# Output stores moved and spaced, attention masks put after the exponential on another engine, and filter taps cast once: one change to an eight-core decoder step

## The chip, the cores and the metric

The kernel runs as one program on all 8 cores of one Trainium2 chip; each core does its own eighth of the tokens. The time is the device time of the slowest core, in microseconds (us). Cores 0 to 3 are one die and cores 4 to 7 the other.

Most executions of one kernel agree within 0.3%. Some fall in a second, slower state, in which the cores of one die (sometimes of both) show a lower granted TensorE clock. Only fast runs are compared here. Where a profile fell in the slow state, the text says which die was undisturbed and uses that one alone.

Engine names in the profile: PE is TensorE, PEld its weight loads, DVE is VectorE, ACT is ScalarE, POOL is GpSimd, SP is SyncE; a q after an engine means its sequencer.

## The reference, cut to what matters

One layer of a hybrid decoder: sliding-window attention with sinks and a gated depthwise convolution run in parallel on the same normed input, are merged by gates, and an MLP follows.

```python
n = rmsnorm(h, norm1_g)
q, k, v, u, g = project(n, w_in)            # u: gated (GLU), 1024 channels
ya = sink_attention(q, k, v)                # blocks of 128 queries see own + previous block
yc = swish(layernorm(depthwise_conv31(u))) @ w_conv_o
h  = h + (g0 * (ya @ w_attn_o) + g1 * yc) @ w_out
h  = h + relu(rmsnorm(h, norm2_g) @ w_up)**2 @ w_down
y  = rmsnorm(h, norm_f_g)
# two request groups: 2 x 8192 prompt tokens, and 128 x 4 sample tokens with KV and conv caches
```

## The kernel before

Each core handles 2048 prompt tokens and 64 sample tokens in three groups (groups 0, 1 and 2 below; 5, 6 and 5 blocks of 128 tokens, the last with the sample tokens). The stages of a group are: k/v/q projections; a loop over 8 channel tiles with the gated projection (`glu`) of tile m and the convolution of tile m-1; gates and branches; output projection; MLP. Work of other kinds is put between the matmuls as side tasks, one for each call of `step()`: the attention units in the conv loop, the next group's first norm in the MLP, and the final norm and the y stores of a group in the k/v/q stage of the next.

A helper records every operation with what it reads and writes, and derives the waits. It tracks SBUF in pieces of 128 bytes, but a DRAM tensor as one whole. So two stores into one output tensor are ordered: the second waits for the landing of the first, on the engine that issues it.

```python
def keys(self, ap):
    name = ap.tensor.name
    if name not in self.base:
        return [name]                  # a DRAM tensor: one key
    ...                                # SBUF: one key for each 128 bytes

# y stores of the group before, one side task each, between the k/v/q matmuls
def out(k):
    if k < 16:
        stt(H[:, k, 0:M], H[:, k, 0:M], v1(V_GF + k), LR[:, 0:M], ALU.mult, ALU.mult)
    if k > 0:
        P.dma("act", yo[g][:, k - 1, :], H[:, k - 1, 0:M], f"d_y{k - 1}")

# scores of an attention unit: the mask is added in PSUM by a product with the identity
for blk in range(2):
    ...
    for hh in range(2):
        b = bank()
        P.op("pe", "matmul", inc=False, out=b[:, :], lhsT=idb[:, :], rhs=msk[...], start=True, stop=False)
        bb.append(b)
    for hh in range(2):
        P.op("pe", "matmul", out=bb[hh][:, :], lhsT=kT[...], rhs=qo[...], start=False, stop=True)
    for hh in range(2):
        act(p[:, :], bb[hh][:, :], AF.Exp, scale=SCALE)

def unit(i, a):                        # scores of this unit, values of the one before
    r = scores(i, a)
    if prev[0]:
        values(*prev[0])
    prev[0] = (i, a, r)

# ... cut ...
def glu(m):
    u = um[m % 3]
    wl = slab()                        # next 1 MB of weights, loaded on GpSimd's queue
    for ci, (c0, n) in enumerate(UC):  # two chunks of columns
        bB = fm(wl, 0, nT, us + c0, n) # 16 matmuls
        step(ci == 0)                  # a unit here in chunk 0
        bA = fm(wl, 1, nT, us + c0, n)
        ...                            # tanh on ACT, product on DVE, into u
        step(ci == 1)                  # and a unit here in chunk 1
    z = ush[m % 2]
    for i in range(4):
        for q in range(4):             # 16 shifted copies, each with its own semaphore
            P.dma("sp", z[32 * i:32 * i + 32, q, 0:L - 3], u[32 * q:32 * q + 32, i:i + L - 3],
                  f"d_ul{m % 2}{i}{q}", merge=(i + q > 0))

def conv(m):                           # 64 small matmuls (96 in the last group)
    z = ush[m % 2]
    P.dma("pool", c_w[:, :, :, :], cwd[m]..., "d_cw")   # taps, cast while loaded
    ...
for m in range(8):
    glu(m)
    if m >= 1:
        conv(m - 1)
```

The taps, the conv temporaries and, in the last group, the sample caches (`KcT`, `vcb`) and the conv state (`stb`) lie in SBUF over the rows of `H` that the y stores still read, so they can be loaded only when those rows have been stored. The caches' loads stand ahead of the last conv loop.

The softmax here doesn't subtract the row's maximum and nothing guards it: scores larger than these inputs give would overflow.

## Time and profile before

| | us |
|---|---|
| median of 4 runs (two of them slow) | 3645.57 (3559.49 to 3942.81) |
| most of its fast runs, over all the rounds below | 3558 to 3592 |
| profiled execution, slowest core | 3556.6 |
| mean span of the 8 cores in it | 3548.2 |

The page of the kernel before begins with busy time by engine; of the 40 slices of the span I show PE's busy tenths and the granted clock.

```profile
span 3556.6 us, 61094 instructions; the slowest of 8 cores (3539.9 to 3556.6 us)
...
PE 3376.2 (95%) x23732; PEld 2172.0 (61%) x23732; DVE 1162.6 (33%) x1846; ACT 705.5 (20%) x1381; POOL 202.3 (6%) x371
...
PE   2999999999999999999999999987999999999994
...
PEclk9999999999999999999999999998999999999997
```

TensorE is the limit. It is idle for 180 us, at the start, in the tail, and in the k/v/q stage of the last group (the 8 and the 7). The list of PE's waits says on whom; its columns are total us, number of times, and the longest.

```profile
PE ps L154 <- DVE R_58 L154: 63.2, 2, 32.8
PE ps L154 <- ACT qo L154: 31.3, 6, 9.1
PE ps L154 <- DMA ush_83<-um_93: 11.1, 3, 5.9
PE ps L154 <- ACT vtok L154: 8.0, 2, 7.0
PE ps L154 <- ACT vst L154: 6.3, 1, 6.3
...
PE ps L154 <- DMA ush_82<-um_93: 2.9, 2, 2.2
```

`R_58` is the first norm. `qo` and `vtok` are the copies of q and v out of PSUM on ACT. What held ACT is in the list of all waits, and its timeline in group 1 shows the pattern (start, us, instruction, and in brackets the idle time before it and who ended it):

```profile
ACT qo L154 <- DMA y<-H: 68.8, 14, 12.8
...
ACT vtok L154 <- DMA y<-H: 45.0, 7, 10.6
```

```profile
1120.92 0.38 ACT L154 ACTIVATE vtok<-ps 128x256 bf16<-128x256 f32 x1 [1.36 <-PE ps L154]
1128.82 0.34 ACTq L154 DMA_DIRECT2D y<-H  x1
1129.26 0.38 ACT L154 ACTIVATE vtok<-ps 128x256 bf16<-128x256 f32 x1 [7.96 <-DMA y<-H]
1139.83 0.34 ACTq L154 DMA_DIRECT2D y<-H  x1
1140.27 0.38 ACT L154 ACTIVATE vtok<-ps 128x256 bf16<-128x256 f32 x1 [10.63 <-DMA y<-H]
```

Each y store sits on ACT until the store before has landed, and the copy behind it waits along. TensorE runs out of PSUM banks and idles, and the granted clock in these stretches is lower, as a table by stretch of these two k/v/q stages shows (the column after POOL is the granted clock):

```profile
1110.00:1190.00 80.00, 65.15 (x399) 40.12 (x397) 16.61 (x18) 10.54 (x25) 2.64 (x5) 0.89 0.63 143
2335.00:2440.00 105.00, 74.19 (x457) 47.20 (x456) 22.17 (x23) 14.95 (x37) 6.76 (x11) 0.84 0.73 157
```

Last, PE's timeline of one attention unit and the convolution after it, in group 0 (core 4).

```profile
189.07 0.59 PE L154 MATMUL ps<-msk,idb 128*128 128x512 bf16 x2
189.59 0.39 PE L154 MATMUL ps<-qo,kT 64*128 64x512 bf16 x2
189.92 0.60 PE L154 MATMUL ps<-msk,idb 128*128 128x512 bf16 x2
190.46 0.39 PE L154 MATMUL ps<-qo,kT 64*128 64x512 bf16 x2
...
191.76 2.38 PE L154 MATMUL ps<-ush_82,cw 128*32 128x320 bf16 x64
```

### The profile page before, as it was taken

The numbers are of one execution on the slowest core, as the hardware profiler recorded it, in microseconds if no ns is written. First come the engines' busy times: TensorE is split into PE (matmuls) and PEld (weight loads), VectorE is DVE, ScalarE is ACT, GpSimd is POOL, SyncE is SP. The second block draws the span as 40 slices with busy tenths as digits, with TensorE's granted clock in tenths as the row PEclk, the third lists the DMA queues.
The fourth block names the chain that finished last, engine by engine and source line by source line (L and its number), as shares of the span: only waits on it lengthen the run. The fifth ranks groups of instructions, "written<-read, shape, count | busy, mean of one in ns | idle before, by whom it ended". The sixth has DMA issues, their size and how long they took to land.

```text
span 3556.6 us, 61094 instructions; the slowest of 8 cores (3539.9 to 3556.6 us)
## 1 busy us (share of the span) xinstructions
PE 3376.2 (95%) x23732; PEld 2172.0 (61%) x23732; DVE 1162.6 (33%) x1846; ACT 705.5 (20%) x1381; POOL 202.3 (6%) x371
## 2 busy tenths in 40 slices
PE   2999999999999999999999999987999999999994
PEld 1656777777776455666666666654566666666663
DVE  4244133332223354224233222333542242222224
ACT  2322133111021333113211011112231131101021
POOL 0000000000000000000000000001100000000000
PEclk9999999999999999999999999998999999999997
DMA  6779877887666666556666655567776666566661
GB/s 135 118 133 174 161 149 152 161 167 136 119 122 134 125 130 143 106 115 118 137 131 132 122 99 104 101 138 156 142 153 114 126 110 113 107 112 114 108 114 71
DMA packets 98474, 453.52 MB, mean 128 GB/s; under 512 B 14960, under 2 KB 27696, under 8 KB 55472
## 3 DMA queue, kind: packets, MB, share of 16 engines
q0 software_dynamic: 51696, 355.75, 56.5%
q1 hardware_dynamic: 39584, 76.56, 8.0%
q10 hardware_dynamic: 6912, 17.30, 1.3%
q8 instruction: 195, 3.19, 0.4%
q14 instruction: 87, 0.71, 0.1%
HBM read 765.00 MB, written 23.85 MB: 222 GB/s over the span
## 4 chain that ended last, share of the span: by engine, by line
PE 89%; DMA 6%; SPq 2%; DVE 1%; issue 1%; ACT 0%; DVEq 0%; ACTq 0%
PE ps L154 89%; DMA y<-H 4%; SPq L154 2%; DMA H<-x 1%; DMA ush_83<-um_93 0%; DVE H L154 0%; DVE rden_67 L154 0%; DMA ush_82<-um_93 0%; DVE nT L154 0%; DVE LR L154 0%; DVE R_58 L154 0%; DMA ush_83<-um_94 0%; DVE um_93 L154 0%; DVE qo L154 0%; SPq L151 0%
## 5 line engine op out<-in xcount | busy, mean ns | idle before, releaser
L154 DVE TENSOR_TENSOR H<-ps,H 128x320 f32<-128x320 f32 (+2 forms) x384 | 201.5, 525 | 566.4 <-PE ps L154 566.2
L154 PE MATMUL ps<-nT,wsl_49 128*128 128x384 bf16 (+2 forms) x1344 | 217.9, 322 | 19.4 <-ACT qo L154 16.9
L154 PE MATMUL ps<-a2T,wsl_50 128*128 128x320 bf16 (+2 forms) x1344 | 203.9, 313 | 0.0
L154 PE MATMUL ps<-hb,wsl_53 128*128 128x320 bf16 (+2 forms) x1344 | 203.9, 313 | 0.0
L154 PE MATMUL ps<-a2T,wsl_51 128*128 128x320 bf16 (+2 forms) x1344 | 203.9, 313 | 0.0
L154 PE MATMUL ps<-hb,wsl_52 128*128 128x320 bf16 (+2 forms) x1344 | 203.9, 313 | 0.0
L154 PEld LDWEIGHTS ps<-nT,wsl_49 128*128 128x128 bf16 x1344 | 133.3, 100 | 101.8 <-issue 33.9
L154 ACT ACTIVATE a2T<-rt_105 128x320 bf16<-128x320 f32 (+2 forms) x96 | 47.6, 496 | 736.1 <-DVE rt_105 L154 736.1
L154 PE MATMUL ps<-nT,wsl_50 128*128 128x352 bf16 (+2 forms) x1152 | 178.9, 316 | 8.6 <-ACT qo L154 8.6
L154 PE MATMUL ps<-nT,wsl_51 128*128 128x352 bf16 (+2 forms) x1152 | 178.2, 315 | 0.5 <-issue 0.5
L154 DVE SCALAR_TENSOR_TENSOR tA<-tA,ps 128x320 f32<-128x320 f32 (+2 forms) x96 | 50.0, 520 | 387.2 <-PE ps L154 386.7
L154 PE MATMUL ps<-hb,wsl_50 128*128 128x320 bf16 (+2 forms) x1152 | 175.3, 313 | 0.0
L154 PE MATMUL ps<-a2T,wsl_49 128*128 128x320 bf16 (+2 forms) x1152 | 174.8, 313 | 0.0
L154 PE MATMUL ps<-a2T,wsl_52 128*128 128x320 bf16 (+2 forms) x1152 | 174.8, 313 | 0.0
L154 PE MATMUL ps<-hb,wsl_51 128*128 128x320 bf16 (+2 forms) x1152 | 174.8, 313 | 0.0
L154 PE MATMUL ps<-a2T,wsl_53 128*128 128x320 bf16 (+2 forms) x1152 | 174.8, 313 | 0.0
L154 PE MATMUL ps<-hb,wsl_49 128*128 128x320 bf16 (+2 forms) x1152 | 174.8, 313 | 0.0
L154 PEld LDWEIGHTS ps<-hb,wsl_52 128*128 128x128 bf16 x1344 | 131.5, 98 | 69.4 <-issue 0.4
L154 PEld LDWEIGHTS ps<-a2T,wsl_50 128*128 128x128 bf16 x1344 | 131.5, 98 | 69.0
L154 PEld LDWEIGHTS ps<-hb,wsl_53 128*128 128x128 bf16 x1344 | 131.5, 98 | 69.0
L154 PEld LDWEIGHTS ps<-a2T,wsl_51 128*128 128x128 bf16 x1344 | 131.5, 98 | 69.0
L154 PE MATMUL ps<-nT,wsl_52 128*128 128x352 bf16 (+2 forms) x960 | 152.5, 320 | 14.3 <-ACT vtok L154 8.0
(222 smaller groups left out, 4284.0 us busy)
## 6 DMA issues: line engine op xcount, KB each, us to landing
wsl_49<-wst POOLq DMA_DIRECT2D x66, 1024.0 KB, 9.5
wsl_50<-wst POOLq DMA_DIRECT2D x66, 1024.0 KB, 9.5
wsl_51<-wst POOLq DMA_DIRECT2D x66, 1024.0 KB, 9.4
wsl_52<-wst POOLq DMA_DIRECT2D x66, 1024.0 KB, 9.8
wsl_53<-wst POOLq DMA_DIRECT2D x66, 1024.0 KB, 9.5
H<-x SPq DMA_DIRECT2D x8, 768.0 KB, 21.6
cw<-cwd POOLq DMA_DIRECT2D x24, 256.0 KB, 8.6
H<-x SPq DMA_DIRECT2D x16, 384.0 KB, 7.2
```

The costliest lines, as they stand in the source:

```text
L154: i = getattr(eng, ins[0])(**ins[1])
```

## The change

It has three parts. The y stores go from ACT to SyncE: eight at once in the side tasks, eight more one by one after each `glu`, in an order that frees the rows needed first; the sample caches are loaded only after tile 5 of the last loop. The 128 mask products on TensorE become 128 affine selects on GpSimd, which set masked exps to zero. The taps are cast to bf16 once, from DRAM to DRAM, and then loaded tile by tile by SyncE into two buffers. With this, the places of the attention units move: one at the end of each chunk, 32 matmuls apart, where they were 48 matmuls apart, then 16 and a convolution.

```diff
+Y_OUT = [0, 1, 2, 3, 4, 10, 11, 12, 5, 6, 7, 8, 9, 13, 14, 15]
@@ taps, behind the first five weight slabs on GpSimd's queue
+        cwb = nc.dram_tensor("cwb", [128, 8, 1024], BF16, kind="Internal").ap()
+        P.dma("pool", cwb[:, :, :], cwd[:, :].rearrange("p (m c) -> p m c", m=8), "d_cwb")
@@ y stores
-            def out(k):
-                if k < 16:
-                    stt(H[:, k, 0:M], H[:, k, 0:M], v1(V_GF + k), LR[:, 0:M], ALU.mult, ALU.mult)
-                if k > 0:
-                    P.dma("act", yo[g][:, k - 1, :], H[:, k - 1, 0:M], f"d_y{k - 1}")
+            def out(i, k):
+                stt(H[:, k, 0:M], H[:, k, 0:M], v1(V_GF + k), LR[:, 0:M], ALU.mult, ALU.mult)
+                stores.append(lambda: P.dma("sp", yo[g][:, k, :], H[:, k, 0:M], f"d_y{k}"))
+                if i < 8:
+                    store()
@@ masks
-                        P.op("pe", "matmul", inc=False, out=b[:, :], lhsT=idb[:, :],
-                             rhs=msk[...].unsqueeze(1).broadcast_to([128, 4, 128]), start=True, stop=False)
+                    bias = v1(V_HB) if first and i == 0 and blk == 0 else 0.0
...
-                        act(p[:, :], bb[hh][:, :], AF.Exp, scale=SCALE)
+                        act(p[:, :], bb[hh][:, :], AF.Exp, scale=SCALE, bias=bias)
+                        d = 1 if blk else -1
+                        v = p[:, :].rearrange("p (g q) -> p g q", g=4)
+                        P.op("pool", "affine_select", out=v, in_=v, pattern=[[0, 4], [d, 128]], base=blk - 1,
+                             channel_multiplier=-d, compare_op=ALU.is_ge, fill=0.0)
@@ conv loop
-                u = um[m % 3]
+                u = um[m % 2]
+                P.dma("sp", cw[m % 2][...], cwb[:, m, :]..., f"d_cw{m % 2}")
...
                     bB = fm(wl, 0, nT, us + c0, n)
-                    step(ci == 0)
                     bA = fm(wl, 1, nT, us + c0, n)
...
-                    step(ci == 1)
+                    step()
...
-                P.dma("pool", c_w[...], cwd[m]..., "d_cw")
...
             for m in range(8):
                 glu(m)
+                store()
+                if last and m == 5:
+                    sample_load()
```

More of the change, by code (lines that the diff above doesn't have):

```diff
@@ L26 @@
 NSLOT = 5
-V_G1, V_G2, V_GF, V_BG, V_CB, V_LG, V_LB, V_SK, V_N = 0, 16, 32, 48, 80, 88, 96, 104, 120
+V_G1, V_G2, V_GF, V_BG, V_CB, V_LG, V_LB, V_SK, V_HB, V_N = 0, 16, 32, 48, 80, 88, 96, 104, 120, 121
 G = 128
@@ L180, in build @@
         wst = din("wst", [110 * 128, 4096])
-        cwd = din("cwd", [8, 128, 1024])
+        cwd = din("cwd", [128, 8192])
         ck = din("ck", [16, 128, 256])
@@ L187, in build @@
         stT = din("stT", [128, 4096])
-        msd = din("msd", [128, 896])
+        msd = din("msd", [128, 512])
         ident = din("ident", [128, 128])
@@ L230, in build @@
         vec = sb("vec", [128, V_N], F32)
-        msk = sb("msk", [128, 896], BF16)
+        msk = sb("msk", [128, 512], BF16)
         idb = sb("idb", [128, 128], BF16)
@@ L249, in build @@
         gt = [over(H, i * 2048, f"gt{i}", [128, 512], F32) for i in range(2)]
-        cw = over(H, 4096, "cw", [128, 4, 8, 32], BF16)
-        um = [over(H, 6144 + i * 2560, f"um{i}", [128, ULEN], BF16) for i in range(3)]
+        cw = [over(H, 4096 + i * 2048, f"cw{i}", [128, 4, 8, 32], BF16) for i in range(2)]
+        um = [over(H, 8192 + i * 2560, f"um{i}", [128, ULEN], BF16) for i in range(2)]
         KcT = over(H, 5 * HB, "KcT", [128, 2, 16, 128], BF16)
@@ L372, in build, with store @@
                 stt(nT[:, k, c], H[:, k, c], v1(V_G1 + k), R1[:, c], ALU.mult, ALU.mult)
+        stores = []
+        def store():
+            if stores:
+                stores.pop(0)()
         def norm1_tasks(g):
@@ L397, in fin @@
                     rstd(LR, S2, c0, n)
-            def out(k):
-                if k < 16:
-                    stt(H[:, k, 0:M], H[:, k, 0:M], v1(V_GF + k), LR[:, 0:M], ALU.mult, ALU.mult)
-                if k > 0:
-                    P.dma("act", yo[g][:, k - 1, :], H[:, k - 1, 0:M], f"d_y{k - 1}")
-            return [fin] + [lambda k=k: out(k) for k in range(17)]
+            def out(i, k):
[3 more added lines that the diff above has]
+                    store()
+            return [fin] + [lambda i=i, k=k: out(i, k) for i, k in enumerate(Y_OUT)]
         for g, (b0, nb, halo, ns) in enumerate(GROUPS):
@@ L464, in scores @@
                 for blk in range(2):
-                    mi = 1 if blk else (0 if first and i == 0 else 2)
-                    bb = []
-                    for hh in range(2):
-                        b = bank()
-                        P.op("pe", "matmul", inc=False, out=b[:, :], lhsT=idb[:, :],
-                             rhs=msk[:, mi * 128:mi * 128 + 128].unsqueeze(1).broadcast_to([128, 4, 128]),
-                             start=True, stop=False)
-                        bb.append(b)
+                    bb = [bank(), bank()]
                     for hh in range(2):
@@ L475, in scores @@
                         P.op("pe", "matmul", out=bb[hh][:, :], lhsT=kT[hs, a, c0 + 128 * blk:c0 + 128 * blk + 128],
-                             rhs=qo[hs, a * 4:a * 4 + 4, c0:c0 + 128], start=False, stop=True)
+                             rhs=qo[hs, a * 4:a * 4 + 4, c0:c0 + 128], start=True, stop=True)
+                    bias = v1(V_HB) if first and i == 0 and blk == 0 else 0.0
                     for hh in range(2):
                         p = pt()
-                        act(p[:, :], bb[hh][:, :], AF.Exp, scale=SCALE)
+                        act(p[:, :], bb[hh][:, :], AF.Exp, scale=SCALE, bias=bias)
[3 more added lines that the diff above has]
+                             channel_multiplier=-d, compare_op=ALU.is_ge, fill=0.0)
                         res[hh, blk] = p
@@ L527, in sample_unit @@
                 pn, pc = pt(), pt()
-                P.op("pe", "matmul", inc=False, out=bn[0:64, 0:256], lhsT=idb[:, 0:64], rhs=msk[:, 640:896],
+                P.op("pe", "matmul", inc=False, out=bn[0:64, 0:256], lhsT=idb[:, 0:64], rhs=msk[:, 256:512],
                      start=True, stop=False)
@@ L532, in sample_unit @@
                 act(pn[0:64, 0:256], bn[0:64, 0:256], AF.Exp, scale=SCALE)
-                P.op("pe", "matmul", inc=False, out=bc[:, 0:256], lhsT=idb[:, :], rhs=msk[:, 384:640],
+                P.op("pe", "matmul", inc=False, out=bc[:, 0:256], lhsT=idb[:, :], rhs=msk[:, 0:256],
                      start=True, stop=False)
@@ L558, in build @@
             if last:
-                sample_load()
                 side += [sample_q] + [lambda a=a, hh=hh: sample_unit(a, hh) for a in range(2) for hh in range(2)]
@@ L573, in glu @@
             def glu(m):
-                u = um[m % 3]
+                u = um[m % 2]
                 wl = slab()
+                P.dma("sp", cw[m % 2][:, :, :, :], cwb[:, m, :].rearrange("p (b t c) -> p b t c", b=4, t=8), f"d_cw{m % 2}")
                 if not first:
@@ L612, in conv @@
                 z = ush[m % 2]
-                c_w = cw
+                c_w = cw[m % 2]
                 A = S1 if m == 0 else cf[m % 2]
-                P.dma("pool", c_w[:, :, :, :], cwd[m].rearrange("p (b t c) -> p b t c", b=4, t=8), "d_cw")
                 for c0, n in PC:
@@ L759, in build @@
         drain()
+        while stores:
+            store()
         P.emit()
@@ L826, in _prep_inputs @@
                 cwd[:, s, c32, :, t, c32] = cwt[j].reshape(8, 4, 32).transpose(2, 0, 1)
-    cwd = cwd.reshape(8, 128, 1024)
-    j = np.arange(128)[:, None]
-    i = np.arange(128)[None, :]
-    m_prev = np.where(j > i, 0.0, NEG).astype(np.float32)
-    m_own = np.where(j <= i, 0.0, NEG).astype(np.float32)
+    cwd = np.ascontiguousarray(cwd.reshape(8, 128, 1024).transpose(1, 0, 2).reshape(128, 8192))
     col = np.arange(256)[None, :]
@@ L836, in _prep_inputs @@
     m_cache = np.where(np.arange(128)[:, None] >= (col % 4) + 1, 0.0, NEG).astype(np.float32)
-    common = dict(ident=np.eye(128, dtype=np.float32), vecs=vecs, cwd=cwd,
+    common = dict(msd=np.concatenate([m_cache, m_new], 1), ident=np.eye(128, dtype=np.float32), cwd=cwd,
                   wst=_slabs(f(w_in)[0], f(w_attn_o)[0], f(w_conv_o)[0], f(w_out)[0], f(w_up)[0], f(w_down)[0]))
@@ L855, in _prep_inputs @@
         d.update(
-            msd=np.concatenate([m_prev if qd > 0 else np.full((128, 128), NEG, np.float32), m_own, m_prev,
-                                m_cache, m_new], 1),
+            vecs=np.where((np.arange(V_N) == V_HB)[None, :] & (qd == 0), np.float32(NEG), vecs),
             ck=np.ascontiguousarray(cK.reshape(16, 128, 256)), cv=np.ascontiguousarray(cV.reshape(16, 128, 256)),
```

## The prediction

> All times are for the fast state (profiled execution of before: 3556.6 us).
>
> **What bounds it now.** TensorE: the page gives PE 95% busy, the chain of waits is 89% PE. Of 180 us of PE idle, 63 us is the first norm and x load, about 45 us the tail. The rest, from the list of PE's waits: 31.3 us on ACT's qo copies, 14.3 on its v copies (vtok 8.0, vst 6.3), about 17 on the shifted conv copies (ush).
>
> **Y stores.** In the timelines of the k/v/q stage of groups 1 and 2, ACT sits between evictions behind its y stores, 2.2 to 13 us apart. Each waits for the landing of the one before: the program tracks a DRAM output as one whole. ACT cannot evict, the PSUM banks fill, PE stops, and the granted clock falls (0.89 and 0.84 in these windows). From the first k matmul to the first mask product: 86.8 us in group 1, 101.8 in group 2; the same matmuls at the undisturbed rate (163, 149, 109 ns for 384, 352, 256 columns) make 66.3 and 62.1. So 60 us is lost. SyncE keeps the chain of landings, but nobody waits for it there. I expect nearly all 60 us back. The final tail (16 stores, 2.3 us each) stays.
>
> **Masks.** In PE's timeline a unit's scores take 1.71 us, 1.07 of it mask products: 32 units, 34 us off a busy PE.
>
> **Added: 128 affine selects on GpSimd** between exp and values. A GpSimd tensor_scalar of 128x512 takes 1.49 us here; the Trainium skill, "GPSIMD Engine Reference", section 3.1, gives 0.77 us for a tight 512-element loop. I estimate 1.2 us. From a unit's scores to its values PE has about 6 us in group 0, 7 in group 1; four selects plus the first exp need about 6. Up to 1.4 us each it hides; at 2 us it would cost some 40 us. Expected loss: 6 us.
>
> **Conv taps.** The loads leave the GpSimd queue, where they waited 89 us for PE, but slab loads never held PE: no gain. The one cast stands behind the first five slabs and ends before the next is needed: 0 us. On SyncE, taps and y stores share the queue with ush copies, whose 16 issues take 10.6 to 12.7 us per channel tile, nearly a loop without attention units. I expect ush waits to grow from 17 to 25 us: loss 8 us.
>
> **Sample caches.** Their load moves behind five late stores. The value cache can start only when y row 9 has landed, about 20 us after the fifth tile, while the first sample unit wants it some 22 us after: PE waits about 8 us there (new).
>
> Sum: 3557 - 60 - 34 + 6 + 8 + 8, about 3485; the losses may partly overlap, so I say 3478 us (-2.2%), range 3440 to 3530. Chances: faster by over 2% 0.62, within 2% 0.35, slower 0.03.
>
> **What would show it.** Right: PE's waits on ACT qo, vtok and vst vanish, the two k/v/q windows shrink to about 67 and 62 us at a clock near 1; 128 matmuls fewer; PE waits for PT on GpSimd under 10 us; a new wait on vcb late in the last conv loop. Wrong: selects of 1.8 us or more with PE waiting for them; ush waits over 40 us; the first PE matmul later than 78 us because of the cast.
>
> **What would make it wrong.** Select time (DVE works in the same stretches and may slow GpSimd), and SyncE's queue becoming the pace of the conv loop.

## The result, and the profile after

The changed kernel took 3523.53 us (median of four, one of them slow; its fast runs lie between 3522.67 and 3524.23). The ratio of fast runs to fast runs of the kernel before is 0.989, with a 95% interval of 0.9861 to 0.9918. A ratio here is always the mean time of one kernel's fast runs over that of the other's in the same rounds, so it is not quite the ratio of medians. The gain is 39 us, half of the 79 us forecast (3557 to 3478), and within 2%.

The page after, and PE's waits in it:

```profile
span 3521.3 us, 61444 instructions; the slowest of 8 cores (3497.6 to 3521.3 us)
...
PE 3345.1 (95%) x23604; PEld 2166.1 (62%) x23604; DVE 1162.4 (33%) x1846; ACT 708.9 (20%) x1381; POOL 266.1 (8%) x476
...
PE   0989999999999999999999999999999999999994
```

```profile
PE ps L155 <- DVE R_58 L155: 81.3, 2, 50.5
PE ps L155 <- DMA ush_83<-um_94: 15.5, 5, 6.4
PE ps L155 <- DMA ush_82<-um_93: 9.3, 2, 5.6
PE ps L155 <- POOL PT_60 L155: 6.5, 1, 6.5
```

The waits on ACT's `qo`, `vtok` and `vst` are gone, and the dip at three quarters of the span too. In their place the first wait has grown by 18 us. The mask products are gone (128 matmuls fewer), and a select is short; this line of the groups by shape gives count, busy time and mean ns:

```profile
L155 POOL TENSOR_SCALAR_AFFINE_SELECT PT_64<-PT_64 128x512 bf16<-128x512 bf16 x16 | 10.1, 634 | 58.1 <-ACT PT_64 L155 58.1
```

To see where the rest went, I cut each core's span by the first matmuls of its stages and took the mean of the eight cores (profiled executions, all fast):

| us | first projection matmul at | group 0 to branches | group 1 | group 2 | tail | span |
|---|---|---|---|---|---|---|
| before | 66.0 | 236.1 | 269.5 | 288.9 | 46.6 | 3548.2 |
| after | 83.1 | 234.8 | 246.4 | 256.8 | 48.0 | 3510.8 |

"Group g to branches" is the k/v/q stage and the conv loop. Splitting it once more, with the marker between the two corrected for the 16 matmuls by which the change moves the first unit:

- k/v/q: 82.6 to 66.3 in group 1, 100.1 to 62.2 in group 2, so -54 us. The two ends are what the prediction computed as undisturbed (66.3 and 62.1).
- conv loops: -2.5 us over the three groups, where the removed mask products alone are 34 us. About 32 us are given back here. (The prediction's sum had 22 of them, as 6 + 8 + 8; what they consist of is the question.)
- start: +17.1 us. Tail: +1.4 us.

Together that is -38 of the -37.4 us measured. So two things have to be explained: the start, and the conv loops.

For the conv loops one more measure is needed: the **conv step**, from the last matmul before a convolution to the first one after it. Mean of 8 cores, tiles 0 to 7:

| us | group 0 | group 1 | group 2 | sum |
|---|---|---|---|---|
| before | 2.64 2.61 2.62 2.61 3.82 7.04 3.49 10.96 | 3.04 3.04 3.04 3.04 3.04 3.09 7.06 5.61 | 3.06 2.97 2.97 2.99 6.58 4.25 5.33 7.19 | 102.1 |
| after | 7.12 3.90 3.94 3.95 3.54 8.65 4.01 8.75 | 4.92 4.36 3.89 3.98 3.97 3.59 4.43 8.68 | 4.85 4.29 4.26 4.38 11.32 5.52 5.49 5.03 | 126.8 |

25 of the 32 us stand in the conv steps. Ten easy tiles, in which before no one waited for anything (tiles 1 to 3 of groups 0 and 2, 1 to 4 of group 1), take 0.9 to 1.4 us longer, 12 us in all. PE's timeline of such a tile after the change (core 7, group 0), to be held against the five lines of before:

```profile
209.14 0.61 PE L155 MATMUL ps<-qo,kT 64*128 64x512 bf16 x4
209.98 0.38 PE L155 MATMUL ps<-PT_60,vtok 128*64 128x512 bf16 x1 [0.24 <-DVE qo L155]
...
211.09 1.11 PE L155 MATMUL ps<-ush_82,cw_91 128*32 128x320 bf16 x3
212.49 2.35 PE L155 MATMUL ps<-ush_82,cw_91 128*32 128x320 bf16 x61 [0.28 <-issue]
```

The first three convolution matmuls take 1.11 us and the other 61 take 2.35. The gap before the 61 is called "issue", time in which the engine waited for nothing that the profile shows, and of the 1.11 us 0.91 count as busy; the two gaps in it, of 0.06 and 0.15 us, are too short to be listed. No list of waits contains this cost: the list gives 24.8 us for `ush` (15.5 + 9.3), close to the 25 forecast, and still the loops lost 32.

### The profile page after: what moved, and what is told of

The parts are those of the page before. It is cut to its first block, busy times and chain, and to the rows that moved or that the text cites. A ratio compares the mean times of both kernels' runs of the same rounds, so it can differ in the third digit from the quotient of the medians.

```text
span 3521.3 us, 61444 instructions; the slowest of 8 cores (3497.6 to 3521.3 us)
## 1 busy us (share of the span) xinstructions
PE 3345.1 (95%) x23604; PEld 2166.1 (62%) x23604; DVE 1162.4 (33%) x1846; ACT 708.9 (20%) x1381; POOL 266.1 (8%) x476
## 4 chain that ended last, share of the span: by engine, by line
PE 88%; DMA 5%; SPq 2%; DVE 2%; issue 1%; another core or an unknown queue 1%; ACT 0%; DVEq 0%; POOL 0%; ACTq 0%; POOLq 0%
PE ps L155 88%; SPq L155 2%; DMA y<-H 2%; DMA H<-x 1%; DMA wsl_53<-wst 1%; DMA ush_83<-um_94 1%; DVE rden_68 L155 1%; DMA ush_82<-um_93 1%; DVE H L155 0%; DMA stb<-stT 0%; DVE LR L155 0%; DVE nT L155 0%; DVE R_58 L155 0%; DVE qo L155 0%
## 5 line engine op out<-in xcount | busy, mean ns | idle before, releaser
L155 PEld LDWEIGHTS ps<-nT,wsl_49 128*128 128x128 bf16 x1344 | 131.7, 98 | 82.0 <-issue 13.5
L155 PE MATMUL ps<-nT,wsl_51 128*128 128x352 bf16 (+2 forms) x1152 | 177.4, 314 | 0.0
L155 PE MATMUL ps<-nT,wsl_50 128*128 128x352 bf16 (+2 forms) x1152 | 176.7, 313 | 0.0
L155 PEld LDWEIGHTS ps<-nT,wsl_51 128*128 128x128 bf16 x1152 | 112.1, 98 | 63.2 <-issue 4.1
```

The costliest lines, as they stand in the source:

```text
L155: i = getattr(eng, ins[0])(**ins[1])
```

## The experiments

Each run was made on one chip beside the kernel before. "Loops" are the three columns "group g to branches" above.

### e1: the cast held back until x has landed

Theory: the cast of the taps (DRAM to DRAM, behind the weight slabs) takes bandwidth from the pieces of x. Rival: the start is late for another reason, for example the changed SyncE work.

```diff
-        P.dma("pool", cwb[:, :, :], cwd[...], "d_cwb")
+        P.dma("pool", cwb[:, :, :], cwd[...], "d_cwb", after=[H[:, 15, half:W0]])
```

> The changed kernel, with the cast of the conv taps held until the last piece of the second half of x has landed. Theory A (the cast's DMA starves the last x pieces and so delays the start): the first matmul on nT moves from 83 us back to about 66 us on the mean of the cores, the whole is 17 us faster than the changed kernel (about 3505 us, ratio to before 0.984), and the conv loops do not change. Rival (the start moved for another reason, for example the order of the x loads or the run itself): the start stays at 83 us and the ratio at 0.989.

Measured: 3508.76 us, ratio 0.9847 (0.9828 to 0.9866). The first projection matmul is back at 65.5 us (after 83.1, before 66.0). Groups 0 and 2 lost 2.4 and 3.1 us of the gain, and the mean span is 3498.0 (after 3510.8). The waits of ACT's first squares on x show the same, before, after, and with the cast held:

```profile
ACT tI L154 <- DMA H<-x: 20.6, 4, 9.5
```

```profile
ACT tI L155 <- DMA H<-x: 37.8, 4, 21.2
```

```profile
ACT tI L155 <- DMA H<-x: 20.2, 4, 9.9
```

In the trace of after, bytes summed by queue in slices of 5 us show SyncE's queue of core 7, which carries x, at 1 to 9 GB/s from 40 to 75 us, while GpSimd's queue carries slabs and cast at 65 to 184 GB/s. (Five other cores have 22 to 33 GB/s on SyncE's queue until 55 us. The queue is slow beside the slabs in the kernel before too, but there they end and the last of x lands at 60 to 62 us; beside the cast it lands at 77 to 80.) The Trainium skill, "DMA: Bandwidth & Descriptors", section "Issuing engines are not separate DMA queues", says that DMAs of all issuers run on the same 16 DMA engines and interleave. A load on another queue was held for 17 us. The start is settled.

### e2: the units back in their old places

Theory: units 32 matmuls apart meet unfinished work of the unit before (VectorE's normalisation takes 0.69 + 3.35 + 0.69 us), and TensorE comes to the convolution without its lead. Rival: SyncE's longer row of work delays the shifted copies.

```diff
                     bB = fm(wl, 0, nT, us + c0, n)
+                    step(ci == 0)
                     bA = fm(wl, 1, nT, us + c0, n)
...
-                    step()
+                    step(ci == 1)
```

> The changed kernel, with the two attention units of a channel tile at their old places (after the first chunk's first product, and at the end). Theory B (with the units 32 matmuls apart, the second unit's values wait for VectorE to free their bank, TensorE's sequencer loses its lead, and the 16 waits of the next conv stand open): the conv step of tiles 1 to 4 falls from about 4 us back to 2.6 to 3.0 us, PE's waits on DVE qo go, and the conv loops together are 12 to 20 us shorter: about 3505 us, ratio 0.984. No wait on the selects appears, since four take 2.5 us. Rival C (the y stores and taps on the SyncE queue delay the ush copies): conv steps stay near 4 us and the time changes by less than 5 us.

Measured (the cast is not held in this one): fast runs 3509.1 to 3514.43 us, ratio 0.9853 (0.9833 to 0.9872). Loops 228.0, 243.0 and 260.0: -6.8, -3.4 and +3.2 against after, so -7 us. The conv steps sum to 111.7 us (after 126.8), with group 0's tiles 1 and 3 at 2.7 and 2.8, group 1's tiles 1 to 4 at 3.0 to 3.1. The places matter, by less than I had thought. Why they matter was still open.

### e3 and e4: the masks alone, in old and in new places

The kernel before with the affine selects only (e3), and with the units in the new places as well (e4). Stores and taps stay as before.

```diff
@@ e3, against before: only the mask part of the change
-                        P.op("pe", "matmul", inc=False, out=b[:, :], lhsT=idb[:, :], rhs=msk[...], ...)
+                        P.op("pool", "affine_select", out=v, in_=v, ...)      # after each exp
@@ e4, on top of it
-                    step(ci == 0)
...
-                    step(ci == 1)
+                    step()
```

> The kernel before with the mask change alone: affine selects, old places of the units, old taps and y stores. If the mask products were worth what PE's timeline showed, 32 units of 1.07 us, the time falls by 28 to 34 us (ratio 0.991 to 0.992). Rival (the shift copies set the period of the conv loop, so shorter units only lengthen the waits for them): it falls by less than 15 us, and waits on ush grow by the difference.

> The kernel before with the mask change and the new places of the units (32 matmuls apart), taps and y stores as before. Theory B: 12 to 20 us slower than the mask change with the old places; conv steps of tiles 1 to 4 near 4 us, though neither y stores nor taps are on SyncE here. Rival C: the same time as with the old places, within 4 us.

Measured: fast runs 3662.73 to 3666.39 us, ratio 1.0281 (1.0261 to 1.0301), and a median of 3658.42 us, ratio 1.0263 (1.0245 to 1.0281). Taking 34 us off TensorE made the kernel 100 us slower. PE's list of waits in e3 has a line that the kernel before does not have (e4 has it too, with 92.7 us):

```profile
PE ps L154 <- DMA cw<-cwd: 96.5, 13, 8.4
```

The tap load is issued on GpSimd's queue, and the selects now stand before it. The conv steps of tiles 0 to 3 in group 0 are 12 to 13 us. This also spoils the pair as a test of the places: with TensorE waiting for taps in most tiles, the places can show nothing (e4 is even a little faster). It shows another thing: the taps' move, which I had booked as "no gain", is what makes the selects possible at all.

### e5: masks and taps, old places, y stores as before

The change without its y part, with the cast held and the units in their old places.

```diff
@@ against before: the mask part, and
-                u = um[m % 3]
+                u = um[m % 2]
+                P.dma("sp", cw[m % 2][...], cwb[:, m, :]..., f"d_cw{m % 2}")
-                P.dma("pool", c_w[...], cwd[m]..., "d_cw")
+        P.dma("pool", cwb[:, :, :], cwd[...], "d_cwb", after=[H[:, 15, half:W0]])
```

> The kernel before with masks as selects and taps through SyncE, the cast held until x has landed, the units at their old places; y stores and sample caches as before. The masks alone cost 100 us because the tap load stood on GpSimd's queue behind the selects and TensorE waited for it. If that was the cause, moving the taps turns it round: no wait on cw, 20 to 30 us faster than before (ratio 0.992 to 0.994), the k/v/q windows still at 83 and 100 us, the start at 66 us. Rival (selects are slow for TensorE in themselves): it stays slower than before.

Measured: ratio 0.9986 (0.9905 to 1.0067); only two runs were fast (3549.6 and 3562.4 us), and the profile fell in the slow state. On the undisturbed die 0 the span is 3531.0 us (before 3547.9 there): -17, by loops 228.0, 260.7 and 288.9 against 236.9, 269.7 and 287.5. No PE wait for taps is left. Groups 0 and 1 give 8.9 and 9.0 us, most of what their mask products cost (10 and 12 units of 1.07 us); group 2 gives nothing.

### e6: the y part alone

The kernel before with the new stores and the late caches; masks, taps and places as before.

```diff
@@ against before
-                    P.dma("act", yo[g][:, k - 1, :], H[:, k - 1, 0:M], f"d_y{k - 1}")
+                stores.append(lambda: P.dma("sp", yo[g][:, k, :], H[:, k, 0:M], f"d_y{k}"))
-                sample_load()
...
                 glu(m)
+                store()
+                if last and m == 5:
+                    sample_load()
```

> The kernel before with the y change alone (stores on SyncE, eight of them in the conv loop, sample caches loaded behind them). The k/v/q windows of groups 1 and 2 fall from 83 and 100 us to 66 and 62 us, 54 us together. If the late cache load costs what the conv step of tile 4 in the last group shows (11.3 against 6.6 us) the conv loops give 4 to 8 us back: 46 to 50 us faster, ratio 0.986. If SyncE's crowding is the main cost of the whole change, they give back 15 us or more: ratio 0.989 or above.

Measured: fast runs 3529.76 to 3531.1 us, ratio 0.9914 (0.9871 to 0.9957). The two k/v/q stages lost 54 us, exactly what they lose in the whole change; but the last loop takes 213.7 us, where it took 188.8. One line holds most of it:

```profile
PE ps L155 <- DMA cw<-cwd: 22.2, 1, 22.2
```

The tap load of tile 4 stands on GpSimd's queue behind the load of the value cache, which waits for y row 9. So here too the parts need each other: the y part without the taps' move gives 25 of its 54 us back.

### e7: cast held and old places together

The edits of e1 and of e2 on the changed kernel, nothing else:

```diff
+        P.dma("pool", cwb[:, :, :], cwd[...], "d_cwb", after=[H[:, 15, half:W0]])
+                    step(ci == 0)
-                    step()
+                    step(ci == 1)
```

> The changed kernel with both mends: the cast held and the units at their old places. If the two effects are independent, they add: 15 us and 10 us off the changed kernel, about 3498 us, ratio 0.981.

Measured: ratio 0.984 (0.97 to 0.998), with two fast runs (3492.6 and 3515.7 us), others slow. On die 0: span 3484.3 us (after 3508.8 there), so -24.5, which is the 17 us of the start plus the 7 of the places. The two corrections add up.

### e8, e9 and e11: the y stores unchained, and the last group's loads in other orders

The stores of different rows need no order among themselves. With `merge=True` they are not chained; thirteen go out in the side tasks, rows 10 to 12 first; the caches load before the last loop (e8). Old places, cast held.

```diff
-Y_OUT = [0, 1, 2, 3, 4, 10, 11, 12, 5, 6, 7, 8, 9, 13, 14, 15]
+Y_OUT = [10, 11, 12, 0, 1, 2, 3, 4, 5, 6, 7, 8, 9, 13, 14, 15]
-                stores.append(lambda: P.dma("sp", yo[g][:, k, :], H[:, k, 0:M], f"d_y{k}"))
-                if i < 8:
+                stores.append(lambda: P.dma("sp", yo[g][:, k, :], H[:, k, 0:M], f"d_y{k}", merge=True))
+                if i < 13:
...
             if last:
+                sample_load()
```

> As the one before, and 13 of the 16 y stores are issued at once, without waiting for one another's landing (each writes its own slice), rows 10 to 12 first, and the sample caches are loaded ahead of the conv loop as in the kernel before. If the late caches and the queue of y stores hold TensorE in the last conv loop, its wait on the selects (4 to 6 us) and on vcb goes, the conv step of tile 4 falls from 12 to about 7 us, and the last loop gets 12 to 18 us shorter; and the final tail, where 16 stores landed one after another in 2.3 us each, falls from 48 us to about 30. Together 25 to 35 us less than with the two mends: ratio about 0.972. If instead the early stores hold the ush copies of the first tiles, the first conv steps of groups 1 and 2 rise by over 3 us.

Measured: 3499.75 us (lowest 3471.75; a die at a lower clock in the others), ratio 0.981 (0.9725 to 0.9895). On die 0 the span is 3467.2 us. The tail fell from 48.0 to 25.9 us, but group 2 stayed at 263.2 us: PE waits 14.5 us (slowest core) for a masked exp, whose select stands behind GpSimd's copy of the conv state, whose load stands behind 4 MB of caches.

e9 loads the caches after tile 1 instead.

```diff
             if last:
-                sample_load()
...
                 store()
+                if last and m == 1:
+                    sample_load()
```

> As the early-y run, with one difference: the sample caches are loaded after the second channel tile of the last conv loop, so the load of the conv state, which GpSimd needs before its first copy and so before the selects queued behind it, is no longer behind them. If GpSimd's in-order queue is what cost the early-y run its gain in the last group, the 16.5 us wait of PE on the selects falls below 2 us and group 2 from its first k matmul to the branches takes 245 to 250 us in place of 263; total about 3452 us on an undisturbed die, ratio 0.970. If the caches' traffic itself was the cost, group 2 stays above 256 us.

Measured: fast runs 3474.24 and 3480.57 us (the other five slow), ratio 0.9724 (0.9661 to 0.9786). The wait for the masked exp fell to 4.6 us, but tile 1's conv step became 20.5 us: its shifted copies land late beside the caches' traffic. Group 2 at 265.4 us: no gain.

e11 keeps e8's order but issues the conv state's load ahead of the caches.

```diff
             if last:
+                P.dma("pool", stb[...], stT[...], "d_st")
                 sample_load()
...
-                P.dma("pool", stb[...], stT[...], "d_st")
```

> The version with the held cast, the old places of the attention units, thirteen unchained early y stores and the sample caches' loads before the last conv loop, with one edit: the load of the conv state is issued ahead of the two cache loads on GpSimd's queue. If the last loop of that version was lost only to the conv state standing behind 4 MB of caches (PE waited 16.5 us for a PT tile behind it), that wait falls to under 4 us, the tile 1 step stays under 6 us as nothing large then lands beside its shifted copies, and group 2 falls from 263 to 245-252 us: 3450-3460 us, ratio 0.967 to 0.972. Rival: the caches' traffic has to be paid beside some tile of the loop wherever it is issued: the wait moves from PT to the shifted copies of tile 0 or 1, group 2 stays at 258-266 us and the ratio at 0.972 to 0.976.

Measured: fast runs 3470.18 and 3470.83 us (the other four slow), ratio 0.9703 (0.9611 to 0.9796). On die 0 of its profile: loops 228.1, 242.9 and 262.8 us. The wait for the masked exp is 3.5 us, and tile 0's conv step is 14.1. So the rival holds: the caches' traffic is paid beside some tile wherever it is issued; issued late, as in the change, it is paid at tile 4 (11.3 us after, 6.6 before).

### e10: the shifted copies issued by two engines

e9 with every second of a tile's shifted copies issued by ScalarE, to test whether SyncE's row of 16 issues (10.6 to 12.7 us long) is the pace of the loop.

```diff
-                        P.dma("sp", z[32 * i:32 * i + 32, q, 0:L - 3], ...
+                        P.dma("act" if i % 2 else "sp", z[32 * i:32 * i + 32, q, 0:L - 3], ...
```

> As the one before, with the 16 shift copies of a channel tile issued half by SyncE and half by ScalarE. If the row of 16 issues on one queue (11 to 13 us a tile) is what sets the pace of tiles without attention units, the conv steps of tiles 5 to 7 fall from 5 to 9 us to about 3 us and the three loops together are 10 to 20 us shorter (ratio 0.965). If the copies' landing under DMA traffic sets it, or ScalarE's own work is delayed by the issues, the gain is under 4 us or a loss.

Measured: ratio 0.98 (0.9755 to 0.9845), fastest run 3482.37 us. Loops 239.4, 248.6 and 259.7 us: against e9 group 0 takes 9.5 us longer, group 1 5 us longer, and group 2 5.7 us less (9.1, 4.4 and -5.7 on the six cores that held their clock in e10's profile). The row of issues is not the only pace, and moving half of it to ScalarE costs more than it saves; which wait it lengthens was not followed up.

### e12: one PSUM bank passed over

By the raw order of bank allocations, the second unit of a tile writes its values to the bank that VectorE still reads for the first. The edit takes one bank out of the ring between the two (on top of e1).

```diff
                     step()
+                    if ci == 0:
+                        bank()
```

> The changed kernel with the held cast (3508.76 us, ratio 0.9847; loops of 237.2, 245.8 and 259.9 us; conv steps of tiles 1 to 3 at 3.9 us in group 0, of tiles 2 to 4 at 3.9 to 4.0 us in group 1) with one edit: one PSUM bank is passed over after the first unit of a channel tile, so that the second unit's values no longer fall on the very bank that VectorE is still reading for the first. If the bank is what takes TensorE's lead in the new places, the conv steps fall to 2.7-3.1 us, groups 0 and 1 lose 7 to 12 us together, group 2 changes by less than 4 us, and the ratio is 0.981 to 0.983. Rival: the new distance itself (units of 32 matmuls, exps and copies then bunched) is what costs, whatever the bank: the conv steps stay at 3.7 us or more, the loops within 3 us, and the ratio at 0.984 to 0.986.

Measured: ratio 0.9828 (0.9744 to 0.9911); the fast runs, 3501.07 to 3533.43 us, differ, as cores 2 and 3 were at a clock of 0.98 in some. Loops 239.1, 246.3 and 257.0 us (e1 237.2, 245.8 and 259.9). On the cores at full clock, conv steps of 3.81 to 3.91 us in group 0's tiles 1 to 3 (e1 3.86 to 3.98) and 3.6 to 3.7 in group 1's tiles 2 to 4 (e1 3.9 to 4.0). My theory missed. It was also a poor test: the trace shows that with the edit the last of the four scores, not the values, falls on the same bank. The reuse was moved ahead by a third of a microsecond, not removed.

The wait records of e1's trace said what to test next. In such a tile (core 4, group 0, tile 2) the first four convolution matmuls start at 192.83, 193.22, 193.66 and 194.10 us, and the waits for 13 of the 16 shifted copies are recorded on these four (2, 3, 4 and 4). In the kernel before (core 3, the same tile) all sixteen are recorded between 189.88 and 191.96 us, on the projection's last matmuls, the mask products, the scores and the values of the unit in front, and the convolution starts at 192.71 us with none open. The Trainium skill, "Perfetto Trace Analysis", section "Tensor Engine Instruction (MATMUL, LD_WEIGHTS)", has the semaphore wait in a queue ahead of the execution, and the profile's start only where the operand read begins; so the profile's busy time would not show the waits. Its section "Identifying Dependency Chains" says that an instruction that waits on several engines may get EventSemaphore instructions put before it. No page that I found gives the cost of a row of them.

The trace does. Its records hold these waits as EVENT_SEMAPHORE instructions of PE's sequencer, which none of the lists and timelines shown here prints. In a row they start 0.106 us apart, before and after the change alike. In the tile of after shown above (core 7, group 0, tile 2) the sequencer passes VectorE's semaphore only at 209.87 us; the waits for the copies then run to 212.38 us, 13 of the 16 on the first four convolution matmuls: 13 times 0.106 is the 1.4 us that the convolution takes longer. They did not wait for bytes: the last of the sixteen copies had landed at 208.03 us, 3 us before the convolution began. In the easy tiles of groups 0 and 1 every copy landed 0.75 us or more before the convolution, on all cores; in those of group 2 they land about as it starts.

### e13: one semaphore for the sixteen copies

The sixteen copies of a tile add to one semaphore, and the convolution waits once, for the full count of 256. The same bytes are waited for. Two other rows get shorter with it: VectorE's next write of the unshifted tile also waits once, and SyncE's first issue follows that write by about 0.12 us, where it took 0.28. (The Trainium skill, "DMA: Bandwidth & Descriptors", section "Why a DMA increments its semaphore by 16 and not by 1", warns that an intermediate value of a shared semaphore does not tell which bytes have landed. Here only the full count is waited for; the result was correct.) On top of e1: new places, cast held.

```diff
-    def dma(self, q, out, in_, sem, merge=False, after=()):
+    def dma(self, q, out, in_, sem, merge=False, after=(), part=(0, 1)):
-        if prev > 0 and self.seen[q].get(sem, 0) < prev:
+        if part[0] == 0 and prev > 0 and self.seen[q].get(sem, 0) < prev:
-        self._commit({sem: self.cnt[sem]}, rk, wk, merge)
+        self._commit({sem: self.cnt[sem] + 16 * (part[1] - 1 - part[0])}, rk, wk, merge)
...
-                              f"d_ul{m % 2}{i}{q}", merge=(i + q > 0))
+                              f"d_ul{m % 2}", merge=(i + q > 0), part=(4 * i + q, 16))
```

> The changed kernel with the held cast (loops of 237.2, 245.8 and 259.9 us over the eight cores, span 3498 us, ratio 0.9847) with one edit: the sixteen shifted copies of a channel tile count up one semaphore instead of sixteen, and the convolution, and VectorE's next write of the unshifted tile, wait once for the full count. Nothing else moves: the units stay in the new places and the same bytes are waited for. If the new places cost what they cost because TensorE then meets the sixteen waits with no lead, the conv steps of tiles 1 to 3 in group 0 fall from 3.9 us to 2.6-2.9, those of tiles 2 to 4 in group 1 from 3.9-4.0 to 3.0-3.3; groups 0 and 1 lose 8 to 16 us together, the span falls to 3478-3490 us and the ratio to 0.979-0.982. Rival: what is waited for is late by itself (VectorE's normalisation, the selects, the landings), whatever the number of waits: the conv steps stay at 3.6 us or more and the span within 4 us of 3498.

Measured: fast runs 3481.4, 3485.14 and 3499.98 us (a fourth slow), ratio 0.9787 (0.9751 to 0.9824). The mean span went from 3498.0 to 3473.5 us: -24.5, more than forecast. Conv steps: 2.61 us in group 0's tiles 1 to 3, 3.04 in group 1's tiles 1 to 4, the floor of before; their sum is 108.2 us (e1 129.7). Ten of the 21.5 us that it fell come from the ten easy tiles; for the others the runs do not separate the convolution's row of waits from VectorE's and SyncE's. The 6 us that still part it from the 102.1 of before are as much as tile 4 of group 2 has grown (12.8 against 6.6), where the caches load. PE's timeline of an easy tile (core 7, group 0):

```profile
205.15 0.61 PE L155 MATMUL ps<-qo,kT 64*128 64x512 bf16 x4
205.99 0.75 PE L155 MATMUL ps<-PT,vtok 128*64 128x512 bf16 x4 [0.24 <-DVE qo L155]
206.46 0.72 PE L155 MATMUL ps<-PT,onesb 128*64 128x512 bf16 x4
207.11 2.37 PE L155 MATMUL ps<-ush,cw 128*32 128x320 bf16 x64
```

The 0.24 us wait for VectorE is still there, unchanged. The convolution behind it is 2.37 us for 64, where after took 3.75 (211.09 to 214.84). So in such a tile 1.4 us were the waits themselves. That the hold by VectorE is what took TensorE's lead away is read from the timelines; no run isolates it.

### e14: one semaphore, old places

The edit of e13 on e7, so that it differs from e13 only by this:

```diff
+                    step(ci == 0)
-                    step()
+                    step(ci == 1)
```

> The same single semaphore in the kernel with the held cast and the old places (loops of 227.4, 241.8 and 260.9 us on an undisturbed die, span 3484.3 us there). If the sixteen waits are all that the places are about, old and new places now come out alike: groups 0 and 1 within 3 us of the run with the new places, conv steps of 2.6-2.9 and 3.0-3.1 us in both, span 3478-3486 us, ratio 0.977-0.981. Rival: the longer distance hides VectorE's and GpSimd's work too: the old places stay better by 5 us or more over groups 0 and 1.

Measured: 3482.99 us, all four runs fast (3480.89 to 3484.43), ratio 0.977 (0.975 to 0.9789). Loops 227.1, 240.2 and 254.9 us, against 225.2, 240.4 and 253.6 in the new places: the same within 2 us. Once the waits are cheap, the places no longer matter. The places had mattered through the waits for the copies.

### e15: one semaphore in the best version

The edit of e13, unchanged, on e11.

> The best version so far (early unchained y stores, conv state first, caches ahead of the last loop, old places, held cast: loops of 228.1, 242.9 and 262.8 us on the undisturbed die, fast runs 3470 us, ratio 0.9703) with the single semaphore. If the waits still cost it something in the tiles whose copies land in time, the loops lose 2 to 8 us and the ratio is 0.967-0.970; the step of tile 0 in group 2 (13.5 us, behind the caches' traffic) stays above 10 us, as it waits for bytes. Rival: with the old places the lead already hides the waits: no change, ratio 0.969-0.972.

Measured: fast runs 3468.55 to 3471.08 us, ratio 0.9735 (0.9718 to 0.9752). The fast runs are those of e11 (3470 us) again. The mean span of die 0 fell from 3465.4 to 3459.0, but the slowest core's time did not: tile 0 of group 2 takes 14.5 us behind the caches' traffic. e11 and e15 are the fastest versions, beating both kernels: some 53 us under the changed one (3523.5 to about 3470).

### e16: a control, one semaphore in the kernel before

The edit of e13, unchanged, on the kernel before.

> A control: the kernel before (span 3548 us; loops of 236.1, 269.5 and 288.9 us; conv steps of tiles 0 to 3 at 2.6 us in group 0, of tiles 0 to 5 at 3.0 us in group 1) with the single semaphore alone. If the single semaphore pays only where TensorE has lost its lead, it gives next to nothing here, as these conv steps are at their floor already: the loops change by less than 3 us each, the ratio is 0.996 to 1.001. Rival: sixteen waits cost time everywhere, hidden until now (on VectorE's writes of the unshifted tile, or in SyncE's order): the loops lose 4 us or more each and the ratio is 0.993 or lower, and then the single semaphore, not the change, brought a part of the gain seen after it.

Measured: two fast runs, 3558.43 and 3552.56 us, too few for an interval (the kernel before beside it: 3560.87 to 3566.72). Loops 236.8, 270.2 and 286.0 us, mean span 3547.2 (before 3548.2). Next to nothing is gained, as expected: only group 2's loop is 2.9 us shorter, with its tiles 5 and 6 at 2.9 and 3.1 us (before 4.3 and 5.3) and its tile 7 longer. In the kernel before, the same sixteen waits were hidden almost everywhere. They are a cost that the change brought out.

## Why the prediction was right or wrong

The bound was right, and both gains were there; the wrong part is two costs put at nothing, each shown by taking it away. With both taken away (e13), the mean span is 3473.5 us, 74.7 under before. That is close to the 79 us forecast, in part by luck: the y stores gave 6 us less than forecast, and 7 of the 79 us were only a guess at how far the losses overlap.

On the mean of the cores 42 us are missing (37.4 for 79). The start is 17 of them, the y stores' term 6, the tail 1. The conv loops are the other 10 to 17: the sum had them 12 us shorter (34 less 22), or 19 with that overlap, and they came 2.5 us shorter.

**Right: TensorE bounds, and the y stores held it through ACT.** The k/v/q stages came to 66.3 and 62.2 us, as computed. ACT's waits on y and PE's waits on `qo`, `vtok` and `vst` vanished. The term was 60 and measured 54, because I read the windows of the slowest core (86.8 and 101.8 us) where the mean of the cores is 82.6 and 100.1. The tail stayed, as said.

**Right: the selects do not hold TensorE by their length.** They take 0.63 us each, half of my estimate of 1.2. (The Trainium skill's figure that I had cited, 0.77 us for a tight loop of 512 elements, was closer than the 1.49 us of the strided tensor_scalar in this trace.) One PE wait for a select is left in the last loop, 6.5 us on the slowest core and 5.9 on the mean. It is a matter of GpSimd's order: the select stands behind a copy that waits for the conv state's load. That it equals the 6 us forecast for slow selects is luck.

**Wrong step: "The one cast stands behind the first five slabs and ends before the next is needed: 0 us."** I asked whom the cast would keep waiting on its own queue, and found nobody. It kept another queue waiting: the last pieces of x came 17 us late (e1 took that back). I had named the sign of it ("the first PE matmul later than 78 us because of the cast"; it was 83), but gave it no weight in the sum.

**Wrong step: "32 units, 34 us off a busy PE", with losses of 6 + 8 + 8 us.** The mask products did leave, but 32 us came back in the conv loops, 25 of them in the conv steps. Only a part of them are the longer waits for copies that I forecast: the listed `ush` waits grew from about 17 to 25 us on the slowest core, just as I wrote, but by 5 on the mean. What the sum did not have at all are the sixteen semaphore waits in front of each convolution: 12 us in the ten tiles that before waited for nothing (4 of them in group 2, where the copies also land later). In the kernel before, TensorE passed them while it still had matmuls to run. With the units closer together and the mask products gone, TensorE arrives with no matmuls in hand, held for a quarter of a microsecond by VectorE, and the waits cost up to 1.4 us a tile. One semaphore in place of sixteen gives 24.5 us (e13; ten of them in those ten tiles), makes the places indifferent (e14), and gives next to nothing to the kernel before (e16). I had costed the removed matmuls as time only, and not as cover.

**Wrong: "slab loads never held PE: no gain" for the taps.** True of the kernel before, but the conclusion that this part is worth nothing is wrong. Without it the selects alone are 100 us slower (e3) and the y part loses 25 us (e6).

**Mis-sized: the sample caches, 8 us as a wait on `vcb`.** The wait hardly appears (0.8 us on e1's slowest core). The cost came as traffic instead, at tile 4 of the last loop: 11.3 us where it was 6.6 (and 12.8 in e13). Moving the loads moved the cost and did not remove it (e8, e9, e11).

What stays open: some 7 of the 32 us stand outside the conv steps; the wait for the select behind the conv state makes 5.9 of them. Of the 25 us in the conv steps, the part outside the ten easy tiles is copies that land late, the caches and rows of waits together, and is not separated. Nor did any run try the ring of PSUM banks with more room, since the edit of e12 did not take the reuse away.

## What to carry to other kernels

Matmuls that are removed may have been cover: before booking their time as a gain, look at what the engine's sequencer does under them, above all a row of semaphore waits. Many small DMAs that are consumed together can count up one semaphore, waited for once at the full total. And ask of each added transfer not only who waits on its queue, but who else is moving bytes at that time: a cast "behind" everything on one queue delayed the start through another.

## What the Trainium skill lacked or had wrong

- "Perfetto Trace Analysis" tells that waits may become extra instructions, but not what a row of them costs when all that it waits for has landed. Here they start 0.106 us apart on TensorE's sequencer, and sixteen of them, when TensorE has no lead, made 64 convolution matmuls take 3.75 us instead of 2.37, of which the profile called only 0.28 us "issue". On VectorE, sixteen such instructions before one write stand 0.068 us apart, 1.1 us in all.
- "DMA: Bandwidth & Descriptors", section "Queues, rings and completion order", has each DMA engine take turns between queues by packet. It does not say how the bytes are then shared: on core 7, beside slabs and cast at 65 to 184 GB/s, the queue of x moved 1 to 9 GB/s for 35 us.
- "GPSIMD Engine Reference" has no time for an affine select: 0.63 us for 128x512 bf16 here, while a strided tensor_scalar of that size took 1.49 us.
